# Projection weights in pieces of 1024 columns, and the residual additions on another engine, in a fused mixer and feed-forward kernel

## The chip, the cores and the metric

The kernel runs on one core of a Trainium2 chip. A core has five engines that run their own instruction streams in order and wait for each other on semaphores: TensorE (PE, matmuls and transposes; PEld is its weight load), VectorE (DVE), ScalarE (ACT), GpSimd (POOL) and SyncE (SP), which here issues every DMA transfer. The metric is the device time of one execution in microseconds. The kernel before takes 2879.96 us, the median of 3 runs (2878.36 to 2882.97).

## The reference

One layer of a trunk, on 2064 tokens (16 meta tokens and 2048 inputs) of width 1024, all in float32:

```python
h = rmsnorm(x, g_pre)
u, q, k, v, o, gi, gf, ga, gb = jnp.split(h @ w_in, IN_SPLITS, axis=-1)
y_a = gelu(s5_ssm(u, ...)); y_a = y_a * sigmoid(y_a @ w_glu)
y_b = head_norm(mlstm_chunkwise(q, k, v, gi, gf)) * sigmoid(o)
merged = sigmoid(ga) * (y_a @ w_a) + sigmoid(gb) * (y_b @ w_b)
x = x + rmsnorm(merged @ w_out, g_post)
# then the channel mixer
h = rmsnorm(x, g_pre); a = causal_dwconv(h @ w_gate, w_conv, b_conv)
return x + rmsnorm((gelu(a) * (h @ w_up)) @ w_down, g_post)
```

`w_glu` is 512 x 512, `w_a` and `w_b` are 512 x 1024, `w_out` is 1024 x 1024.

## The kernel before

A float32 product is made from three matmuls on rounded halves (`mm3`): each operand is split into a high part in a short float format and the low rest. The split of a weight piece is `split_w`: ScalarE copies the float32 piece `ws` into `wh` (line 140), VectorE subtracts to get `wl` (line 142, or line 144 where a factor is applied too). `load_w` puts the load of `ws` ahead of it (line 149). The three tiles `ws`, `wh` and `wl` lie in the pool `dw` with two buffers each, and every weight of the kernel goes through them: 1024 columns wide in the dense stages, 512 wide in the projections that the change touches.

The program goes through these stages. Up to about 978 us: the input projection, the state-space scan and the mLSTM, which leave `ya`, `yb`, the gates `gab_d` and so on in DRAM. From there to about 1464 us: four blocks `b` of 512 tokens (the first has two more), each with `glu(b)` (4 weight pieces), `branches(b)` (8 pieces of `w_b` and 8 of `w_a`, one pair for each 128 output channels `m`) and `out_proj(b)` (2 halves `nh` of 8 pieces `k`, each used for four tiles of 128 tokens, 12 matmuls of 512 columns). Then `out_post(b, i)` for each tile of 128 tokens: a norm (its power runs on GpSimd, line 105), a scaling on VectorE (line 1020), the addition of the residual `xt` (line 1021), and a store to `h1_d` (line 1022). The residual piece is loaded into `xh`, of which there are three buffers (line 1018). The posts of block `b - 1` are issued after the branches of block `b`, so they stand beside `out_proj(b)`; those of block 3 come at the end, and add on VectorE. `norm_block` turns `h1_d` into the transposed, normed `h2_d`.

The feed-forward part multiplies with a seven-product scheme, in two passes `p` over 1024 tokens each. Its operands are sums and differences of quarters of `h2_d`, loaded in halves `hf` into the `mk` tiles (three buffers, lines 1039 and 1040): `ops_first` makes three differences (lines 1058 to 1060) and splits four operands (lines 1047 and 1048), `ops_second` makes three more (lines 1072 to 1075). `ops_first(0)` stands in the program behind `out_proj(3)`, and its work is spread over `branches(3)` and `out_proj(3)`. The feed-forward units start at about 1464 us and run to about 2380; the down projection follows to the end.

The order of the instructions on each engine is not written out by hand: the framework sets it when the program is built, from a simulated timeline, and it is fixed from then on. A change of a size or of an engine in one stage thus reorders the stages around it.

Of the kernel before, what the change touches and what calls it, by code (L numbers as in the profile page):

```python
# [49 lines left out]
def mixer_ffn_kernel(  # L50
# [1 line left out]
    tc: tile.TileContext,  # L52
    x, meta, h0_t, g_mix_pre, g_mix_post, w_v, w_g, w_m, b_gates,
    lam_re, lam_im, log_dt, sb, sb_sw, sc, sc_sw, ssm_d,
    w_glu, conv_qk, b_qk, g_head, w_a, w_b, w_out,
    g_ffn_pre, g_ffn_post, w_gate, w_up, conv_f, b_f, w_down,
    out,
    stop=None,
# [855 lines left out]
    def glu(b):  # L914
        ts, n, pieces, rowt = blkC[b]
        yaT, yah, yal = ya[b]
        y2h, y2l = t4(4), t4(5)
        for m in range(4):
            wh, wl = load_w(dw, w_glu[m], 512)
            for p0, pn in pieces:  # L920
                ps = pst("mm", [128, pn])
                for k in range(4):
                    mm3(ps, wh[:, k], wl[:, k], yah[:, k, p0:p0 + pn], yal[:, k, p0:p0 + pn], k == 0, k == 3)
                tg = cr.tile([128, 512], F32, tag="tg", name="tg", bufs=2)
                S.activation(tg[:, :pn], ps, AF.Tanh, scale=0.5)
                V.scalar_tensor_tensor(tg[:, :pn], tg[:, :pn], 1.0, yaT[:, m, p0:p0 + pn], ALU.add, ALU.mult)
                S.activation(y2h[:, m, p0:p0 + pn], tg[:, :pn], AF.Copy)
                V.tensor_tensor(y2l[:, m, p0:p0 + pn], tg[:, :pn], y2h[:, m, p0:p0 + pn].bitcast(F32), ALU.subtract)
        y2[b] = (y2h, y2l)
# [16 lines left out]
    def branches(b):  # L946
        ts, n, pieces, rowt = blkC[b]
        y2h, y2l = y2[b]
        ybh, ybl = yb2[b]
        mh, ml = [t4(8), t4(9)], [t4(10), t4(11)]  # L950
        for m in range(8):
            bh, bl = load_w(dw, w_b[m], 512, 0.25)
            ah, al = load_w(dw, w_a[m], 512, 0.25)
            gat = cr.tile([128, 2, 514], F32, tag="gat", name="gat", bufs=2)
            P.dma_start(out=gat[:, 0, :n], in_=gab_d[m, :, ts:ts + n])
            P.dma_start(out=gat[:, 1, :n], in_=gab_d[8 + m, :, ts:ts + n])
            for p0, pn in pieces:
                pc = slice(p0, p0 + pn)
                pb = pst("mm", [128, pn])
                for k in range(4):  # L960
                    mm3(pb, bh[:, k], bl[:, k], ybh[:, k, pc], ybl[:, k, pc], k == 0, k == 3)
                V.scalar_tensor_tensor(gat[:, 1, pc], gat[:, 1, pc], 1.0, pb, ALU.add, ALU.mult)
                pa = pst("ac", [128, pn])
                for k in range(4):
                    mm3(pa, ah[:, k], al[:, k], y2h[:, k, pc], y2l[:, k, pc], k == 0, k == 3)
                V.scalar_tensor_tensor(gat[:, 0, pc], gat[:, 0, pc], 1.0, pa, ALU.add, ALU.mult)
                V.tensor_tensor(gat[:, 0, pc], gat[:, 0, pc], gat[:, 1, pc], ALU.add)
                mhm = mh[m // 4][:, m % 4, pc]
                S.activation(mhm, gat[:, 0, pc], AF.Copy)
                done = V.tensor_tensor(ml[m // 4][:, m % 4, pc], gat[:, 0, pc], mhm.bitcast(F32), ALU.subtract)  # L970
        mg[b] = (mh, ml)
        return done
# [3 lines left out]
    def out_proj(b):  # L976
# [3 lines left out]
        for nh in range(2):  # L980
# [1 line left out]
            for i, (c0, rows) in enumerate(rowt):  # L982
                pss[i] = pst("mm" if rows == 2 else "ac", [rows, 512])
            for k in range(KD):
                wh, wl = load_w(dw, w_out[k * 128:(k + 1) * 128, nh * 512:(nh + 1) * 512], 512)
                wh = wh.rearrange("p a b -> p (a b)")
                wl = wl.rearrange("p a b -> p (a b)")
                for i, (c0, rows) in enumerate(rowt):
                    mm3(pss[i], mh[k // 4][:, k % 4, c0:c0 + rows], ml[k // 4][:, k % 4, c0:c0 + rows], wh, wl,
                        k == 0, k == KD - 1)  # L990
# [9 lines left out]
    def out_post(b, i):  # L1000
# [11 lines left out]
        for hh in range(2):  # L1012
# [5 lines left out]
                P.dma_start(out=xt[:rows], in_=src[:, cs_])  # L1018
            o = o2[hh]
            V.scalar_tensor_tensor(o[:rows], o[:rows], rs[:rows], g2b[:rows, cs_], ALU.mult, ALU.mult)  # L1020
            (V if b == 3 else G).tensor_tensor(o[:rows], o[:rows], xt[:rows], ALU.add)
            P.dma_start(out=h1_d[ts + c0:ts + c0 + rows, cs_], in_=o[:rows])

    def norm_block(b, pl):
# [25 lines left out]
    def ops_first(p):  # L1050

        op = {n: (t4(2 * i), t4(2 * i + 1)) for i, n in enumerate((1, 6, 2, 7))}
        for hf in range(2):
            b11, b12 = op_load(p, hf, 0)
            op_split(op[1], p, hf, b11)
            b21, b22 = op_load(p, hf, 1)
            E = V if p else G
            E.tensor_tensor(b11, b12, b11, ALU.subtract)
            E.tensor_tensor(b12, b22, b12, ALU.subtract)
            E.tensor_tensor(b22, b22, b11, ALU.subtract)  # L1060
            op_split(op[6], p, hf, b22)
            op_split(op[2], p, hf, b21)
            op_split(op[7], p, hf, b12)
# [236 lines left out]
def layouts(i):  # L1300
# [7 lines left out]
    def stat(mat, k):  # L1308
# [26 lines left out]
        "sc": st(cre, cim),  # L1335
        "sc_sw": st(cim, cre),
        "ssm_d": a["ssm_d"][0].T,
        "w_glu": stat(a["w_ssm_glu"][0], 4),
        "conv_qk": conv(a["w_qk_conv"][0], 8),
        "b_qk": a["b_qk_conv"].reshape(8, 128).T,  # L1340
        "g_head": row("g_head_norm"),
        "w_a": stat(a["w_branch_ssm"][0], 4),
        "w_b": stat(a["w_branch_mlstm"][0], 4),
        "w_out": a["w_out"][0],
        "g_ffn_pre": a["g_ffn_pre"].reshape(8, 128).T,
        "g_ffn_post": row("g_ffn_post"),
# [27 lines left out]
```

## Time and profile before

The profiled execution took 2886.44 us, of which 2884.7 are the span from the first to the last instruction; the granted TensorE clock was 0.99 on average.

| | busy us | share of the span | instructions |
|---|---|---|---|
| TensorE, matmuls (PE) | 2794.8 | 97% | 15654 |
| TensorE, weight loads (PEld) | 2506.7 | 87% | 15654 |
| VectorE (DVE) | 1798.8 | 62% | 3508 |
| ScalarE (ACT) | 1047.4 | 36% | 1995 |
| GpSimd (POOL) | 183.2 | 6% | 257 |

A row of instructions reads: line of the kernel, engine, operation, output <- inputs by the program's names, shapes, count | busy us, mean ns of one | idle time of the engine just before them and what ended it. `A <- B` in a list of waits means that A waited for B. A time that stands in brackets behind a row of the timeline is the idle time before it, with what ended it. Of a wait for several things only the one that came last is named.

### The profile page before, as it was taken

How to read it: one execution, taken by the hardware profiler on the slowest of the kernel's cores; microseconds unless marked ns; L12 is line 12 of the kernel's file. 1: busy time of each engine (PE TensorE's matmuls, PEld its weight loads, DVE VectorE, ACT ScalarE, POOL GpSimd, SP SyncE). 2: the span in 40 equal slices, each digit the busy share in tenths (PEclk: the TensorE clock that was granted, in tenths of full speed). 3: DMA queues.
4: the chain of work that ended last, by engine and by line, in shares of the span. 5: the costliest groups of instructions: out<-in, count | busy, mean ns of one | idle time of the engine just before them, and what ended most of it. 6: DMA issues, size and time to landing. Idle time of an engine off the chain costs nothing.

```text
span 2884.7 us, 41374 instructions
## 1 busy us (share of the span) xinstructions
PE 2794.8 (97%) x15654; PEld 2506.7 (87%) x15654; DVE 1798.8 (62%) x3508; ACT 1047.4 (36%) x1995; POOL 183.2 (6%) x257
## 2 busy tenths in 40 slices
PE   8999999999999999998779999998999999999999
PEld 8999999999999987776579999996888888888887
DVE  4638897377555465576777777788777774224333
ACT  6102233233443444434344444444444443223221
POOL 1000000000000000212310000001000000000000
PEclk9999999999999999999989999999999999999999
DMA  8334453211454564676746222224222235334553
GB/s 303 105 73 137 169 162 117 74 69 70 147 158 134 159 200 134 196 221 219 234 142 201 80 81 84 71 82 175 81 84 78 87 98 179 95 99 146 166 168 125
DMA packets 328442, 389.74 MB, mean 135 GB/s; under 512 B 41569, under 2 KB 230390, under 8 KB 328114
## 3 DMA queue, kind: packets, MB, share of 16 engines
q1 hardware_dynamic: 328242, 387.10, 41.9%
q8 instruction: 123, 2.02, 0.3%
q14 instruction: 77, 0.63, 0.1%
HBM read 282.90 MB, written 104.12 MB: 134 GB/s over the span
## 4 chain that ended last, share of the span: by engine, by line
PE 83%; DMA 7%; DVE 6%; issue 2%; ACT 1%; POOL 1%; SPq 0%; POOLq 0%; DVEq 0%; ACTq 0%
PE mm L158 9%; PE mm L156 9%; PE mm L157 9%; PE ac L157 8%; PE ac L158 8%; PE ac L156 8%; PE ac L162 5%; PE ac L163 5%; PE ac L161 5%; PE mm L163 4%; PE mm L162 4%; PE mm L161 4%; DMA mk<-h_d 1%; DMA wo_d<-W 1%; DMA h_d<-mk 1%
## 5 line engine op out<-in xcount | busy, mean ns | idle before, releaser
L158 PE MATMUL mm<-hTh,wl 128*128 128x410 f32 (+3 forms) x1216 | 430.4, 354 | 0.0
L156 PE MATMUL mm<-hTh,wh 128*128 128x410 f32 (+3 forms) x1216 | 429.4, 353 | 0.1
L157 PE MATMUL mm<-hTl,wh 128*128 128x410 f32 (+3 forms) x1216 | 427.2, 351 | 0.0
L1275 DVE TENSOR_TENSOR yhl<-ys,yhl 128x1024 fp32r<-128x1024 f32 (+1 forms) x96 | 109.1, 1137 | 293.7 <-ACT yhl L1274 293.7
L157 PE MATMUL ac<-t,yhl 128*128 128x512 f32 x704 | 278.5, 396 | 0.0
L158 PE MATMUL ac<-t,yhl 128*128 128x512 f32 x704 | 277.3, 394 | 0.0
L156 PE MATMUL ac<-t,yhl 128*128 128x512 f32 x704 | 276.6, 393 | 0.0
L161 PE MATMUL mm<-t,w 128*128 128x258 f32 (+2 forms) x792 | 254.6, 322 | 12.6 <-ACT w L1142 9.7
L161 PE MATMUL ac<-t,w 128*128 128x258 f32 (+2 forms) x792 | 255.0, 322 | 12.1 <-ACT t L1047 8.0
L162 PE MATMUL mm<-t,w 128*128 128x258 f32 (+2 forms) x792 | 255.1, 322 | 1.3 <-DVE t L1048 1.3
L162 PE MATMUL ac<-t,w 128*128 128x258 f32 (+2 forms) x792 | 254.9, 322 | 1.1 <-DVE t L1048 1.1
L163 PE MATMUL mm<-t,w 128*128 128x258 f32 (+2 forms) x792 | 253.6, 322 | 1.7 <-DVE w L1143 1.7
L163 PE MATMUL ac<-t,w 128*128 128x258 f32 (+2 forms) x792 | 254.7, 322 | 0.0
L140 ACT ACTIVATE wh<-ws 128x512 fp32r<-128x512 f32 (+1 forms) x176 | 124.5, 708 | 317.7 <-PE mm L157 139.3
L156 PEld LDWEIGHTS mm<-hTh,wh 128*128 128x128 f32 x1216 | 229.2, 188 | 3.2 <-DVE ev L351 0.8
L157 PEld LDWEIGHTS mm<-hTl,wh 128*128 128x128 f32 x1216 | 229.2, 189 | 2.6
L158 PEld LDWEIGHTS mm<-hTh,wl 128*128 128x128 f32 x1216 | 229.2, 189 | 2.4
L1274 ACT ACTIVATE yhl<-ys 128x1024 fp32r<-128x1024 f32 (+1 forms) x96 | 94.8, 988 | 350.6 <-PE ac L157 349.0
L1142 ACT ACTIVATE w<-s 128x512 fp32r<-128x512 f32 x176 | 110.3, 630 | 192.5 <-PE ac L163 112.3
L161 PEld LDWEIGHTS mm<-t,w 128*128 128x128 f32 x792 | 151.0, 191 | 25.6 <-ACT w L1142 9.9
L161 PEld LDWEIGHTS ac<-t,w 128*128 128x128 f32 x792 | 150.7, 190 | 25.1 <-ACT t L1047 8.3
L142 DVE TENSOR_TENSOR wl<-ws,wh 128x512 fp32r<-128x512 f32 (+1 forms) x112 | 104.5, 936 | 108.4 <-ACT wh L140 108.1
(448 smaller groups left out, 6180.2 us busy)
## 6 DMA issues: line engine op xcount, KB each, us to landing
ys<-y_d SPq DMA_DIRECT2D x64, 512.0 KB, 3.7
wg<-in_w_gate_dram SPq DMA_DIRECT2D x44, 512.0 KB, 4.8
wu<-in_w_up_dram SPq DMA_DIRECT2D x44, 512.0 KB, 3.9
gab_d<-ev SPq DMA_DIRECT2D x80, 205.0 KB, 2.2
ws<-in_w_m_dram SPq DMA_DIRECT2D x32, 512.0 KB, 4.0
ws<-in_w_out_dram SPq DMA_DIRECT2D x64, 256.0 KB, 3.0
gat<-gab_d SPq DMA_DIRECT2D x48, 256.0 KB, 3.6
ys<-y_d SPq DMA_DIRECT2D x32, 384.0 KB, 3.1
```

Of the source, the lines that this page charges most:

```text
L140: S.activation(wh, ws, AF.Copy, scale=scale)
L142: V.tensor_tensor(wl, ws, wh.bitcast(F32), ALU.subtract)
L156: T.matmul(out=ps, lhsT=lh, rhs=rh, start=first, stop=False)
L157: T.matmul(out=ps, lhsT=lh, rhs=rl, start=False, stop=False)
L158: T.matmul(out=ps, lhsT=ll, rhs=rh, start=False, stop=last)
L161: T.matmul(out=ps, lhsT=lh, rhs=rh, start=first, stop=False, skip_group_check=True)
L162: T.matmul(out=ps, lhsT=lh, rhs=rl, start=False, stop=False, skip_group_check=True)
L163: T.matmul(out=ps, lhsT=ll, rhs=rh, start=False, stop=last, skip_group_check=True)
L1142: S.activation(t[:, 0], src, AF.Copy)
L1274: S.activation(yh, ys, AF.Copy)
L1275: V.tensor_tensor(yl, ys, yh.bitcast(F32), ALU.subtract)
```

## The change

It has two parts.

The weights of the three projections are fetched and split 1024 columns at a time. `w_glu` is laid out on the host so that two of its pieces lie side by side, and is loaded at every second `m`. `w_b` and `w_a` are joined into `w_ba`, one load for each `m`. Of `w_out` one transfer fetches two row blocks `k` side by side. There are half as many loads and splits (72 instead of 144), each of twice the width; the buffers stay two. The matmuls read the same halves of the same numbers.

The additions of two tensors on GpSimd move to VectorE: the residual addition of blocks 0 to 2 and the three differences of `ops_first(0)`, each done twice. What stays on GpSimd in these stages is the power of the norm and the small memsets.

```diff
         for m in range(4):
-            wh, wl = load_w(dw, w_glu[m], 512)
+            if m % 2 == 0:
+                w2h, w2l = load_w(dw, w_glu[m // 2], D)
+            wh, wl = (t[:, m % 2 * 4:m % 2 * 4 + 4] for t in (w2h, w2l))
...
         for m in range(8):
-            bh, bl = load_w(dw, w_b[m], 512, 0.25)
-            ah, al = load_w(dw, w_a[m], 512, 0.25)
+            bah, bal = load_w(dw, w_ba[m], D, 0.25)
+            (bh, bl), (ah, al) = ((bah[:, i:i + 4], bal[:, i:i + 4]) for i in (0, 4))
...
             for k in range(KD):
-                wh, wl = load_w(dw, w_out[k * 128:(k + 1) * 128, nh * 512:(nh + 1) * 512], 512)
-                wh = wh.rearrange("p a b -> p (a b)")
-                wl = wl.rearrange("p a b -> p (a b)")
+                if k % 2 == 0:
+                    ws = dw.tile([128, D], F32, tag="ws", name="ws")
+                    P.dma_start(out=ws.rearrange("p (k n) -> p k n", k=2),
+                                in_=w_out[k * 128:(k + 2) * 128, nh * 512:(nh + 1) * 512].rearrange(
+                                    "(k p) n -> p k n", k=2))
+                    w2 = split_w(dw, ws, D)
+                wh, wl = (t[:, k % 2 * 512:k % 2 * 512 + 512] for t in w2)
...
-            (V if b == 3 else G).tensor_tensor(o[:rows], o[:rows], xt[:rows], ALU.add)
+            V.tensor_tensor(o[:rows], o[:rows], xt[:rows], ALU.add)
...
-            E = V if p else G
-            E.tensor_tensor(b11, b12, b11, ALU.subtract)
-            E.tensor_tensor(b12, b22, b12, ALU.subtract)
-            E.tensor_tensor(b22, b22, b11, ALU.subtract)
+            V.tensor_tensor(b11, b12, b11, ALU.subtract)
+            V.tensor_tensor(b12, b22, b12, ALU.subtract)
+            V.tensor_tensor(b22, b22, b11, ALU.subtract)
```

In the changed kernel's listing the line numbers behind `glu` are higher: 1020 and 1021 become 1026 and 1027, 1022 and 1018 become 1028 and 1024, 1048 becomes 1054, 1058 to 1060 become 1063 to 1065, 1072 becomes 1077. The loads of `w_out` are at 989 instead of 149.

The first place where the order moves is VectorE beside `out_proj(3)`. `o` are the output tiles, `t` the operands of the feed-forward part, `mk` the halves of `h2_d`. Before, from the third split of a `w_out` piece on:

```order
L142 TENSOR_TENSOR wl<-ws,wh 128x512
L103 TENSOR_SCALAR ms<-sq 128x1
L142 TENSOR_TENSOR wl<-ws,wh 128x512
L1020 SCALAR_TENSOR_TENSOR o_12999<-o_12999,rs,g2b 128x512
L1020 SCALAR_TENSOR_TENSOR o_13155<-o_13155,rs,g2b 128x512
L103 TENSOR_SCALAR ms<-sq 128x1
L1048 TENSOR_TENSOR t_14244<-mk,t_14243 128x1028
L1072 TENSOR_TENSOR mk<-mk 128x2x514
L1048 TENSOR_TENSOR t_14240<-mk,t_14239 128x1028
L1048 TENSOR_TENSOR t_14242<-mk,t_14241 128x1028
L142 TENSOR_TENSOR wl<-ws,wh 128x512
```

Now, from the third split (of a piece of twice the width) to just ahead of the fourth:

```order
L142 TENSOR_TENSOR wl<-ws,wh 128x1024
L1065 TENSOR_TENSOR mk<-mk 128x2x514
L1026 SCALAR_TENSOR_TENSOR o_12699<-o_12699,rs,g2b 128x512
L1026 SCALAR_TENSOR_TENSOR o_12831<-o_12831,rs,g2b 128x512
L103 TENSOR_SCALAR ms<-sq 128x1
L1054 TENSOR_TENSOR t_13812<-mk,t_13811 128x1028
L1077 TENSOR_TENSOR mk<-mk 128x2x514
L1027 TENSOR_TENSOR o_12699<-o_12699,xh 128x512
L1054 TENSOR_TENSOR t_13808<-mk,t_13807 128x1028
L1027 TENSOR_TENSOR o_12831<-o_12831,xh 128x512
L1026 SCALAR_TENSOR_TENSOR o_12701<-o_12701,rs,g2b 128x512
L1026 SCALAR_TENSOR_TENSOR o_12833<-o_12833,rs,g2b 128x512
```

Two rows follow (`L103` and a fourth `L1054`), and then the fourth split. The additions `L1027` and the difference `L1065` stand now between two splits on the engine that makes the splits; a split covers twice as many matmuls.

The second place is SyncE's queue at the same point, where the h1 stores, the residual loads and the weight loads stand in one line. Before:

```order
L1022 DMA h_d<-o_12999 128x512
L1018 DMA xh<-in_x_dram 128x512
L1022 DMA h_d<-o_13155 128x512
L1018 DMA xh<-in_x_dram 128x512
L1040 DMA mk<-h_d 128x2x1026 x2
L149 DMA ws<-in_w_out_dram 128x512
L1022 DMA h_d<-o_13001 128x512
L1018 DMA xh<-in_x_dram 128x512
L149 DMA ws<-in_w_out_dram 128x512
```

Now:

```order
L989 DMA ws<-in_w_out_dram 128x2x512
L1046 DMA mk<-h_d 128x2x1026
L1028 DMA h_d<-o_12699 128x512
L1024 DMA xh<-in_x_dram 128x512
L1028 DMA h_d<-o_12831 128x512
L1024 DMA xh<-in_x_dram 128x512
L1046 DMA mk<-h_d 128x2x1026
L989 DMA ws<-in_w_out_dram 128x2x512
L1028 DMA h_d<-o_12701 128x512
L1024 DMA xh<-in_x_dram 128x512
L989 DMA ws<-in_w_out_dram 128x2x512
```

A store waits for its addition, and what stands behind it waits too. Five of the eight loads of `w_out` now stand ahead of the first store; before, six of the sixteen did, of half the width.

More of the change, by code (lines that the diff above doesn't have):

```diff
@@ L54, in mixer_ffn_kernel @@
     lam_re, lam_im, log_dt, sb, sb_sw, sc, sc_sw, ssm_d,
-    w_glu, conv_qk, b_qk, g_head, w_a, w_b, w_out,
+    w_glu, conv_qk, b_qk, g_head, w_ba, w_out,
     g_ffn_pre, g_ffn_post, w_gate, w_up, conv_f, b_f, w_down,
@@ L1337, in layouts @@
         "ssm_d": a["ssm_d"][0].T,
-        "w_glu": stat(a["w_ssm_glu"][0], 4),
+        "w_glu": stat(a["w_ssm_glu"][0], 4).reshape(2, 2, 128, 512).transpose(0, 2, 1, 3).reshape(2, 128, 1024),
         "conv_qk": conv(a["w_qk_conv"][0], 8),
@@ L1341, in layouts @@
         "g_head": row("g_head_norm"),
-        "w_a": stat(a["w_branch_ssm"][0], 4),
-        "w_b": stat(a["w_branch_mlstm"][0], 4),
+        "w_ba": np.concatenate([stat(a["w_branch_mlstm"][0], 4), stat(a["w_branch_ssm"][0], 4)], axis=2),
         "w_out": a["w_out"][0],
```

## The prediction

> **What bounds the kernel now.** I read the engines' shares first, then the chain of work that ended last. These two lines of the page say that TensorE (PE) sets the end:
>
> ```profile
> PE 2794.8 (97%) x15654; PEld 2506.7 (87%) x15654; DVE 1798.8 (62%) x3508; ACT 1047.4 (36%) x1995; POOL 183.2 (6%) x257
> ...
> PE 83%; DMA 7%; DVE 6%; issue 2%; ACT 1%; POOL 1%; SPq 0%; POOLq 0%; DVEq 0%; ACTq 0%
> ```
>
> The diff leaves the number of matmuls as it is, so time can come only from TensorE's gaps: 2884.7 - 2794.8 = 90 us of the span, and matmuls at a low clock beside them. The third view is busy time by stretches, cut at the stages of the projections (about 978 to 1464 us). The columns are the stretch, its width, busy us of PE, PEld, DVE, ACT and POOL with their counts, the clock granted to TensorE, the DMA share and GB/s.
>
> ```profile
> 978.00:1045.00 67.00, 62.11 (x485) 60.83 (x484) 49.27 (x109) 37.02 (x69) 0.00 (x0) 0.95 0.79 233
> 1045.00:1158.00 113.00, 112.59 (x511) 86.21 (x510) 55.89 (x93) 49.33 (x91) 0.00 (x0) 1.00 0.48 146
> 1158.00:1215.00 57.00, 52.76 (x228) 40.80 (x227) 32.95 (x54) 18.53 (x34) 19.33 (x15) 1.00 0.68 217
> 1215.00:1270.00 55.00, 54.83 (x252) 43.14 (x251) 39.13 (x68) 29.80 (x59) 3.05 (x5) 1.00 0.62 193
> 1270.00:1335.00 65.00, 58.99 (x267) 46.34 (x266) 38.58 (x65) 24.64 (x46) 18.02 (x19) 1.00 0.81 259
> 1335.00:1400.00 65.00, 57.55 (x233) 43.85 (x232) 45.71 (x60) 28.33 (x51) 10.46 (x4) 0.97 0.50 165
> 1400.00:1464.00 64.00, 49.97 (x196) 38.07 (x195) 36.59 (x45) 20.15 (x32) 21.72 (x18) 0.89 0.67 226
> 1464.00:1500.00 36.00, 20.73 (x130) 19.94 (x129) 32.85 (x56) 18.05 (x38) 8.28 (x6) 0.72 0.46 161
> 2000.00:2100.00 100.00, 100.00 (x432) 80.93 (x431) 72.33 (x113) 40.69 (x65) 4.56 (x5) 1.00 0.25 85
> ```
>
> The gaps lie where POOL has work: the stretches with 10 to 22 us of POOL lack 4.2, 6.0, 7.5 and 14.0 us of PE, while 1045 to 1158 and 1215 to 1270, with 0 and 3 us of it, lack 0.4 and 0.2. The last row prices an undisturbed matmul of 512 columns: 100 / 432 = 0.2315 us. The stretches 1335 to 1400 and 1400 to 1464 hold only such matmuls, so they need 233 x 0.2315 = 53.9 and 196 x 0.2315 = 45.4 us: 11.1 and 18.6 us are lost there, the lower clock included. What TensorE waits for from 960 to 1620 (us, times, longest):
>
> ```profile
> PE ac L157 <- DVE wl L142: 11.8, 8, 4.8
> PE mm L161 <- ACT w L1142: 9.7, 1, 9.7
> PE ac L156 <- ACT wh L140: 8.1, 6, 2.8
> PE mm L156 <- ACT wh L140: 5.0, 7, 2.3
> ...
> PE ac L161 <- ACT u L1185: 3.9, 1, 3.9
> ```
>
> The first, third and fourth are the split weight pieces, 24.9 us; the 9.7 and the 3.9 belong to the start of the feed-forward units behind 1464.
>
> Why pieces come late is in the timeline. One POOL row (a pair of L1058), then VectorE's rows under it, and one row from later for comparison:
>
> ```profile
> 1355.99 5.34 POOL L1058 TENSOR_TENSOR mk<-mk 128x1028 f32<-128x1028 f32 x2 [25.35 <-DVE t L1048]
> ```
>
> ```profile
> 1359.39 2.50 DVE L967 TENSOR_TENSOR gat<-gat 128x512 f32<-128x512 f32 x1
> 1361.80 0.67 DVE L962 SCALAR_TENSOR_TENSOR gat<-gat,mm 128x512 f32<-128x512 f32 x1
> 1362.40 2.26 DVE L144 SCALAR_TENSOR_TENSOR wl<-ws,wh 128x512 fp32r<-128x512 f32 x1
> ...
> 1382.08 0.68 DVE L144 SCALAR_TENSOR_TENSOR wl<-ws,wh 128x512 fp32r<-128x512 f32 x1
> ```
>
> Beside POOL's additions a VectorE instruction with two SBUF inputs takes 2.3 to 2.5 us instead of 0.68; L962, which reads one input from PSUM, keeps 0.67. The Trainium skill ("SBUF — State Buffer", Who interferes with whom) says the same: such an instruction and a GpSimd one that reads SBUF exclude each other, and the later one blocks. By that page alone the moved additions' whole time could be VectorE time given back, which leads to the first rival below; the groups' rows bound it lower.
>
> The second cause is SyncE's queue. In out_proj(3) ScalarE stood 13.28 us for a weight piece, and the queue had stood for POOL's additions (here the waits of SP from 1400 to 1464):
>
> ```profile
> 1429.67 0.63 ACT L140 ACTIVATE wh<-ws 128x512 fp32r<-128x512 f32 x1 [13.28 <-DMA ws<-in_w_out_dram]
> ```
>
> ```profile
> SPq L1022 <- POOL o L1021: 9.9, 5, 4.3
> ```
>
> **The additions.** POOL loses these groups (978 to 1500; 2 more of two rows):
>
> ```profile
> L1021 POOL TENSOR_TENSOR o<-o,xh 128x512 f32<-128x512 f32 x24 | 38.9, 1633 | 14.4 <-DVE o L1020 10.6 <-DMA xh<-in_x_dram 2.8 <-issue 1.1
> L1058 POOL TENSOR_TENSOR mk<-mk 128x1028 f32<-128x1028 f32 x2 | 5.3, 2693 | 25.4 <-DVE t L1048 25.4
> L1059 POOL TENSOR_TENSOR mk<-mk 128x1028 f32<-128x1028 f32 x2 | 5.2, 2616 | 3.6 <-DMA mk<-h_d 3.6
> L1060 POOL TENSOR_TENSOR mk<-mk 128x1028 f32<-128x1028 f32 x2 | 4.3, 2168 | 0.1
> ```
>
> VectorE's prices (978 to 1600):
>
> ```profile
> L142 DVE TENSOR_TENSOR wl<-ws,wh 128x512 fp32r<-128x512 f32 x79 | 64.8, 823 | 105.1 <-ACT wh L140 104.9
> L144 DVE SCALAR_TENSOR_TENSOR wl<-ws,wh 128x512 fp32r<-128x512 f32 x64 | 46.8, 731 | 14.6 <-ACT wh L140 14.0
> L1020 DVE SCALAR_TENSOR_TENSOR o<-o,rs,g2b 128x512 f32<-128x512 f32 x32 | 24.3, 800 | 8.8 <-POOL rs L105 8.8
> L1021 DVE TENSOR_TENSOR o<-o,x 128x512 f32<-128x512 f32 x8 | 5.2, 685 | 0.0
> L1072 DVE TENSOR_TENSOR mk<-mk 128x1028 f32<-128x1028 f32 x2 | 4.6, 2302 | 0.0
> L1074 DVE TENSOR_TENSOR mk<-mk 128x1028 f32<-128x1028 f32 x2 | 2.5, 1227 | 0.2 <-DMA mk<-h_d 0.2
> ```
>
> Added: 26 x 0.685 + 6 x 1.227 = 25 us. Given back against the undisturbed 0.685 and 1.227: 79 x 0.138 + 64 x 0.046 + 32 x 0.115 + 2 x 1.075 = 10.9 + 2.9 + 3.7 + 2.2 = 20 us, and a few more in smaller groups. VectorE's load stays even. What changes is latency: an addition of 1.6 us becomes 0.7, and the h1 store and the x load behind it leave SyncE that much sooner. The price: VectorE is in order, so where an x piece or an h2 half hasn't landed, the splits behind it wait too.
>
> **The pieces.** Undisturbed 1024-column pieces (dense stages, 300 to 980), the 512-column one of this stage, and three loads:
>
> ```profile
> L142 DVE TENSOR_TENSOR wl<-ws,wh 128x1024 fp32r<-128x1024 f32 x23 | 28.1, 1222 | 2.4 <-ACT wh L140 2.4
> ```
>
> ```profile
> L140 ACT ACTIVATE wh<-ws 128x1024 fp32r<-128x1024 f32 x23 | 24.4, 1061 | 30.0 <-PE mm L157 30.0
> ```
>
> ```profile
> L140 ACT ACTIVATE wh<-ws 128x512 fp32r<-128x512 f32 x143 | 89.9, 630 | 192.9 <-DMA ws<-in_w_out_dram 77.3 <-PE ac L158 40.0 <-PE ac L157 21.1
> ```
>
> ```profile
> ws<-in_w_m_dram SPq DMA_DIRECT2D x32, 512.0 KB, 4.0
> ws<-in_w_out_dram SPq DMA_DIRECT2D x64, 256.0 KB, 3.0
> xh<-in_x_dram SPq DMA_DIRECT2D x24, 256.0 KB, 4.8
> ```
>
> There are two buffers of each kind before and after. A piece's split can start when the piece two back is used up, and must be done when the one between is: 12 x 0.2315 = 2.78 us before, of which 0.63 + 0.69 = 1.3 is work, so 1.5 us of delay was free. Now it is 5.56 us, less 1.06 + 1.22 = 2.3: 3.3 us is free. The load behind it is covered by 5.56 us for 4.0 instead of 2.78 for 3.0. The work of the splits is the same.
>
> **The sum.** Out_proj(3), 18.6 lost. The longest VectorE run between two splits in the new order is L1065, four L1026, three L1054, L1077 and two L1027: 5 x 1.227 + 6 x 0.685 = 10.2 us, with the split itself 11.5. It has 5.56 + 3.3 = 8.9 of cover, so it stalls TensorE 2.6 us; I add 2 for the powers on GpSimd (a pair of L1026 waits for one) and for ScalarE, and 1.5 at low clock. Some 6 us stay, 12.5 are won. Glu and branches(3), 11.1 lost: the run is two L1054, four of L1063 to L1065 and an L972, 6 x 1.227 + 0.685 = 8.0 us, behind two pieces already split (11.1 us of matmuls), which stalls nothing; I leave 3.5 for the stage's head and win 7.5. The two earlier out_projs, 10.2 of plain gaps: a run of eight 512-column instructions is 5.5 us, two powers lengthen it by about 2, against 3.3 free; half stays, 5 are won. The head (978 to 1045, 4.9 missing) and the feed-forward start (15.3 missing) have the same instructions in nearly the same order: 0, with 3 us either way. Together 25 us: the profiled execution's 2886.4 becomes 2861, and the median of the runs, 2880.0 (6.4 below the profiled one), becomes **2855 us**.
>
> Ends for what the trace doesn't show: the standing of VectorE at its new loads costs nothing if each lands in time, and at most 26 us (the last rival); the removed contention is worth at least the 4.2 + 6.0 gaps' half and at most everything that is missing.
>
> **The rivals.** *More comes back.* All of 11.1 + 18.6 + 10.2 = 40 us goes and the feed-forward start shrinks by 4, since VectorE reaches it earlier: 2836. For it: 1045 to 1158 shows these stages with no gap. Against it: the run of 11.5 us. *The heads pay.* At the start of a stage nothing is split ahead; a piece's first matmul then comes (4.0 - 3.0) + (1.06 - 0.63) + (1.22 - 0.69) = 2 us later. With 12 heads (glu, branches and out_proj of four blocks) that is 24 us, which cancels the gain: 2879. Against it: the next stage's first pieces stand directly behind the last w_out piece in SyncE's order. The Trainium skill ("Perfetto Trace Analysis", Optimizing Scalar/DVE Operations) speaks for this one: where these engines aren't saturated but cause bubbles elsewhere, it advises smaller instructions, and the change makes larger ones; VectorE is at 62%. *VectorE waits in POOL's place (slower).* An x buffer comes round after addition, issue and landing, 0.7 + 0.7 + 4.8 = 6.2 us for three additions, and VectorE's work for three is 6 x 0.685 = 4.1; 26 / 3 rounds stand 2.1 us each, 18 us, and the h2 halves that POOL awaited 3.6 us stand twice, 7: 26 us with the splits behind them. Of the gain only the deeper prefetch stays, some 14 of the three weight waits' 24.9: 2880 + 12 = 2892. It decides once over 14 us of that standing reaches TensorE. Against it: the first three x pieces are loaded ahead, and two buffered pieces cover 8.9 us.
>
> **How the numbers follow.** Forecast 0.62 (its own range 2845 to 2867), more comes back 0.15, the heads pay 0.16, VectorE waits 0.07. The 8-in-10 range is 2836 to 2874: it takes in the second case and half of the way to the third. A measurement here tells 0.2% (5.8 us) from no change. Faster by more than that: 0.62 + 0.15 + a third of the heads' 0.16 = 0.82; within it 0.10; slower 0.08, the last rival with a rest of the heads'.
>
> **What would show it.** Right: no L1021-like rows on POOL; two-input VectorE rows at 0.69 and 1.22 throughout; TensorE short of less than 4 us in glu and branches(3) and of about 5 in out_proj(3); ScalarE's wait for w_out far below 13 us; the span up to 978 and behind 1600 as before. Wrong: VectorE idle before its additions for x loads by more than 10 us in all, TensorE's waits for wl as long as now, or a feed-forward start longer by what was won.

## The result, and the profile after

The changed kernel takes 2849.84 us, the median of 4 runs (2847.5 to 2852.07), against 2879.94 us for the kernel before on the same chip (4 runs, 2878.36 to 2882.97): a ratio of 0.9894, with a 95% interval of 0.9877 to 0.9911. The change is worth 30.1 us; the forecast was 25 (2855 us). The profiled execution took 2852.07 us, of which 2850.3 are the span, 34.4 less than the span before. The two profiled executions lie 6.5 us (before) and 2.2 us (now) above the medians of their kernels, so 4.3 of these 34.4 us are a difference of executions and not of kernels.

These are the engines' shares and the chain of waits of the changed kernel, from its page:

```profile
PE 2785.3 (98%) x15654; PEld 2509.1 (88%) x15654; DVE 1790.8 (63%) x3468; ACT 1035.4 (36%) x1923; POOL 132.0 (5%) x225
...
PE 84%; DMA 7%; DVE 6%; issue 1%; ACT 1%; POOL 0%; SPq 0%; DVEq 0%; POOLq 0%; ACTq 0%
```

GpSimd lost 51 us of work, VectorE gained none (1798.8 before, 1790.8 now), and TensorE's gaps went from 90 to 65 us. To see where, I cut both spans at the same events: the end of ScalarE's last eviction in `out_proj(0)`, `(1)` and `(2)`, and the first feed-forward matmul. Between two of these lie the posts, `out_proj`, `glu` and branches of one block. The busy time by such stretches, of the kernel before and then of the changed one (the columns are those of the prediction's table of stretches):

```profile
1109.30:1218.50 109.20, 104.55 (x448) 81.47 (x447) 67.75 (x108) 49.50 (x92) 19.33 (x15) 1.00 0.62 193
1218.50:1335.80 117.30, 111.12 (x506) 87.28 (x505) 77.62 (x132) 51.92 (x99) 21.06 (x24) 1.00 0.74 235
1335.80:1464.40 128.60, 107.12 (x425) 81.60 (x424) 82.70 (x105) 48.08 (x82) 32.19 (x22) 0.93 0.58 193
sum 355.10, PE 322.78 PEld 250.35 DVE 228.07 ACT 149.50 POOL 72.57; mean PE 107.59 PEld 83.45 DVE 76.02 ACT 49.83 POOL 24.19
```

```profile
1104.90:1211.20 106.30, 103.36 (x453) 82.83 (x452) 68.49 (x101) 46.03 (x73) 5.99 (x5) 1.00 0.65 203
1211.20:1322.00 110.80, 108.12 (x485) 86.95 (x484) 74.06 (x116) 48.43 (x82) 8.07 (x13) 0.98 0.69 226
1322.00:1430.90 108.90, 104.09 (x445) 83.26 (x444) 80.36 (x109) 45.12 (x64) 9.74 (x11) 0.97 0.70 244
sum 326.00, PE 315.56 PEld 253.03 DVE 222.91 ACT 139.58 POOL 23.79; mean PE 105.19 PEld 84.34 DVE 74.30 ACT 46.53 POOL 7.93
```

The three blocks together have nearly as many matmuls as before (1379 and 1383 recorded), and take 355.1 - 326.0 = 29.1 us less: 2.9, 6.5 and 19.7. Their gaps fell from 32.3 to 10.4 us. Ahead of 1109 us 4.4 us were won, behind the feed-forward start 0.9 (1420.3 us to the end before, 1419.4 now).

What TensorE waits for in the changed kernel from 960 to 1590 (us, times, longest):

```profile
PE ac L161 <- ACT u L1190: 8.6, 2, 6.4
PE mm L161 <- ACT w L1147: 5.9, 1, 5.9
PE ac L157 <- DVE wl L142: 5.6, 5, 3.5
...
PE ac L158 <- DVE wl L144: 0.7, 1, 0.7
PE ac L156 <- ACT wh L140: 0.5, 1, 0.5
```

The waits for split weight pieces, 24.9 us in the forecast's count, are 5.6 + 0.7 + 0.5 = 6.8 us. (The count before left out the waits for the subtractions with a factor, line 144: 4.8 us, which the 6.8 take in. With them it was 29.7.) What stands first now is the feed-forward start, which the change did not touch.

VectorE's groups in the changed kernel from 978 to 1466 us show what became of the stretched rows:

```profile
L142 DVE TENSOR_TENSOR wl<-ws,wh 128x1024 fp32r<-128x1024 f32 x39 | 47.6, 1221 | 73.5 <-ACT wh L140 73.5
L144 DVE SCALAR_TENSOR_TENSOR wl<-ws,wh 128x1024 fp32r<-128x1024 f32 x32 | 39.1, 1222 | 16.2 <-ACT wh L140 16.2
L1026 DVE SCALAR_TENSOR_TENSOR o<-o,rs,g2b 128x512 f32<-128x512 f32 x32 | 22.6, 745 | 2.9 <-POOL rs L105 2.0 <-POOL mk L1045 0.9
...
L1027 DVE TENSOR_TENSOR o<-o,xh 128x512 f32<-128x512 f32 x24 | 16.3, 685 | 8.7 <-DMA xh<-in_x_dram 8.7
```

Each of these groups of two-input rows is at its undisturbed time (1.22, 0.745, 0.685), and VectorE's standing for the residual loads is 8.7 us in all.

The one long wait that is left is the predicted one. VectorE's rows between the third and the fourth split of `out_proj(3)`, and the matmul behind:

```profile
1388.79 1.22 DVE L142 TENSOR_TENSOR wl<-ws,wh 128x1024 fp32r<-128x1024 f32 x1
1389.92 1.23 DVE L1065 TENSOR_TENSOR mk<-mk 128x1028 f32<-128x1028 f32 x1
1391.58 1.41 DVE L1026 SCALAR_TENSOR_TENSOR o<-o,rs,g2b 128x512 f32<-128x512 f32 x2 [0.44 <-POOL rs L105]
...
1400.13 1.22 DVE L142 TENSOR_TENSOR wl<-ws,wh 128x1024 fp32r<-128x1024 f32 x1
```

```profile
1401.40 0.79 PE L157 MATMUL ac<-wl,t 128*128 128x512 f32 x1 [3.54 <-DVE wl L142]
```

From split to split it is 11.3 us (11.5 forecast), and TensorE stands 3.54. Two stretches of the changed kernel, `out_proj(3)` from its first matmul to the feed-forward start, and the 6 us behind that wait:

```profile
1380.10:1430.90 50.80, 47.26 (x193) 37.91 (x192) 35.65 (x53) 20.28 (x28) 9.43 (x8) 0.93 0.78 275
1401.40:1407.40 6.00, 6.00 (x15) 4.70 (x16) 4.36 (x7) 0.60 (x1) 3.00 (x3) 0.52 0.61 193
```

Its 192 matmuls need 192 x 0.2315 = 44.4 us, so 6.4 are lost: 3.5 in the wait, and 6.0 - 15 x 0.2315 = 2.5 behind it, where the granted clock is 0.52.

### The profile page after: what moved, and what is told of

Same layout as the page of the kernel before. It is cut to its first block, busy times and chain, and to the rows that moved or that the text cites. A ratio compares the mean times of both kernels' runs of the same rounds, so it can differ in the third digit from the quotient of the medians.

```text
span 2850.3 us, 40942 instructions
## 1 busy us (share of the span) xinstructions
PE 2785.3 (98%) x15654; PEld 2509.1 (88%) x15654; DVE 1790.8 (63%) x3468; ACT 1035.4 (36%) x1923; POOL 132.0 (5%) x225
## 4 chain that ended last, share of the span: by engine, by line
PE 84%; DMA 7%; DVE 6%; issue 1%; ACT 1%; POOL 0%; SPq 0%; DVEq 0%; POOLq 0%; ACTq 0%
PE mm L156 9%; PE mm L158 9%; PE mm L157 9%; PE ac L157 9%; PE ac L158 9%; PE ac L156 9%; PE ac L161 5%; PE ac L163 5%; PE ac L162 5%; PE mm L162 4%; PE mm L163 4%; PE mm L161 4%; DMA gat<-gab_d 1%; DMA wo_d<-W 1%; DMA h_d<-mk 1%
## 5 line engine op out<-in xcount | busy, mean ns | idle before, releaser
L1280 DVE TENSOR_TENSOR yhl<-ys,yhl 128x1024 fp32r<-128x1024 f32 (+1 forms) x96 | 109.2, 1138 | 295.3 <-ACT yhl L1279 295.3
L140 ACT ACTIVATE wh<-ws 128x1024 fp32r<-128x1024 f32 x104 | 109.8, 1058 | 239.4 <-PE mm L157 140.1
L1147 ACT ACTIVATE w<-s 128x512 fp32r<-128x512 f32 x176 | 110.4, 631 | 202.5 <-PE ac L163 119.3
L161 PEld LDWEIGHTS ac<-t,w 128*128 128x128 f32 x792 | 151.1, 191 | 30.0 <-ACT u L1190 9.7
L162 PEld LDWEIGHTS ac<-t,w 128*128 128x128 f32 x792 | 151.6, 191 | 13.3 <-DVE t L1054 1.8
```

The source lines that it names most:

```text
L140: S.activation(wh, ws, AF.Copy, scale=scale)
L161: T.matmul(out=ps, lhsT=lh, rhs=rh, start=first, stop=False, skip_group_check=True)
L162: T.matmul(out=ps, lhsT=lh, rhs=rl, start=False, stop=False, skip_group_check=True)
L1147: S.activation(t[:, 0], src, AF.Copy)
L1280: V.tensor_tensor(yl, ys, yh.bitcast(F32), ALU.subtract)
```

## The experiments

All runs beside the kernel before on the same chip, in three groups with a before of their own (2883.74, 2881.45 and 2881.21 us). The gain is the difference of the medians.

| run | us, median (range) | ratio to before (95%) | gain |
|---|---|---|---|
| pieces only | 2861.11 (2858.06 to 2864.65) | 0.9924 (0.9912 to 0.9936) | 22.6 |
| additions only | 2869.51 (2866.42 to 2874.71) | 0.9953 (0.9941 to 0.9966) | 14.2 |
| residual additions only | 2873.23 (2872.02 to 2873.35) | 0.9963 (0.9949 to 0.9977) | 10.5 |
| idle additions on GpSimd | 2862.58 (2857.33 to 2864.17) | 0.9924 (0.9912 to 0.9937) | 21.2 |
| split in halves | 2849.87 (2846.41 to 2855.38) | 0.9888 (0.9871 to 0.9905) | 31.6 |
| stores on another queue | 2877.35 (2875.0 to 2880.63) | 0.9985 (0.9976 to 0.9993) | 4.1 |
| differences on GpSimd | 2852.47 (2847.53 to 2855.4) | 0.989 (0.9872 to 0.9908) | 29.0 |
| later norms and evictions | 2841.24 (2837.72 to 2844.28) | 0.9856 (0.984 to 0.9872) | 40.2 |
| changed kernel again | 2850.04 (2846.39 to 2855.08) | 0.989 (0.9873 to 0.9907) | 31.2 |
| wide pieces for w_out only | 2855.22 (2852.86 to 2855.78) | 0.9906 (0.9892 to 0.9921) | 26.0 |
| later norms only | 2843.18 (2840.64 to 2846.78) | 0.9867 (0.9852 to 0.9882) | 38.0 |
| norms apart | 2843.59 (2842.1 to 2848.01) | 0.987 (0.9855 to 0.9885) | 37.6 |

The same cuts as above, from each run's trace, in us. Single executions of one kernel differ by some us (the changed kernel's runs reach from 2846.4 to 2855.1), so differences of 2 or 3 here say nothing alone. The last two columns belong together: a run that is longer in block 3 is often shorter behind it (the pieces alone have 9.6 us more than the changed kernel in block 3 and 7.5 less from the feed-forward start).

| run | end of out_proj(0) | block 1 | block 2 | block 3 | from the feed-forward start |
|---|---|---|---|---|---|
| before | 1109.3 | 109.2 | 117.3 | 128.6 | 1420.3 |
| changed | 1104.9 | 106.3 | 110.8 | 108.9 | 1419.4 |
| changed again | 1103.0 | 107.9 | 110.7 | 108.2 | 1419.5 |
| pieces only | 1105.6 | 111.1 | 112.2 | 118.5 | 1411.9 |
| additions only | 1106.0 | 108.6 | 114.3 | 120.6 | 1418.0 |
| residual additions only | 1105.3 | 107.0 | 115.0 | 128.4 | 1415.8 |
| idle additions | 1101.5 | 113.6 | 113.1 | 116.9 | 1416.5 |
| split in halves | 1102.9 | 102.7 | 108.2 | 117.2 | 1419.3 |
| another queue | 1106.4 | 108.3 | 118.2 | 122.8 | 1417.5 |
| differences on GpSimd | 1104.3 | 108.1 | 110.4 | 111.9 | 1418.9 |
| later norms and evictions | 1100.0 | 107.3 | 110.8 | 107.9 | 1416.3 |
| w_out only | 1106.9 | 105.0 | 112.2 | 114.9 | 1414.8 |
| later norms only | 1100.2 | 108.0 | 111.6 | 106.6 | 1414.4 |
| norms apart | 1105.4 | 105.9 | 112.1 | 109.1 | 1413.6 |

### Each part alone

The pieces alone are the changed kernel with both additions back:

```diff
-            V.tensor_tensor(o[:rows], o[:rows], xt[:rows], ALU.add)
+            (V if b == 3 else G).tensor_tensor(o[:rows], o[:rows], xt[:rows], ALU.add)
...
-            V.tensor_tensor(b11, b12, b11, ALU.subtract)
+            E = V if p else G
+            E.tensor_tensor(b11, b12, b11, ALU.subtract)
```

(with the other two differences alike). Expected:

> The changed kernel with the additions of the residual and of the three differences back on GpSimd; the pieces stay 1024 wide. The forecast's theory: three causes, of which this leaves one removed, the shallow prefetch. The three weight waits of TensorE were 24.9 us before; the deeper prefetch is worth some 14 of them (the figure of the last rival), so about 2866; VectorE's two-input rows beside GpSimd's additions stay at 1.5 to 2.5 us. Rival A, depth is all: the pieces alone give the whole 30 us, 2850, and the stretched rows don't matter since a split covers 5.56 us of matmuls. Rival B, GpSimd is all: no gain, 2875 to 2880, since a wider split beside an addition is stretched by the same factor as two narrow ones.

The additions alone are the kernel before with these lines the other way round. Expected:

> The kernel before with both groups of additions on VectorE; the pieces stay 512 wide. The forecast's theory: contention and the standing of SyncE's queue are gone, 1.5 us of free delay per piece remain, and the runs of VectorE instructions between two splits (5.5 to 10 us) now meet the shallow prefetch: about half of the gain, 2864. Rival A, depth is all: nothing, 2878 or more, since a run of eight 512-column instructions (5.5 us) stalls TensorE by some 2 us wherever it stands. Rival B, GpSimd is all: the whole gain, 2850.

Measured: 22.6 and 14.2 us. Neither rival holds: both parts give something alone, the pieces more than I had put on them (22.6 instead of 14), the additions somewhat less (14.2 instead of 16). Their sum is 36.8, more than the 30 or 31 of both together, so some 6 us are waits that either part removes. In the trace of the pieces alone, VectorE's rows beside GpSimd's additions in `out_proj(3)`, TensorE's wait for them, and the group of the scalings from 1050 to 1460 us:

```profile
1405.61 3.15 DVE L1026 SCALAR_TENSOR_TENSOR o<-o,rs,g2b 128x512 f32<-128x512 f32 x2 [4.09 <-POOL rs L105]
...
1408.75 2.25 DVE L1054 TENSOR_TENSOR t<-mk,t 128x1028 fp32r<-128x1028 f32 x1
1410.93 2.32 DVE L1078 TENSOR_TENSOR mk<-mk 128x1028 f32<-128x1028 f32 x1
...
1416.84 4.43 DVE L142 TENSOR_TENSOR wl<-ws,wh 128x1024 fp32r<-128x1024 f32 x2
```

```profile
PE ac L157 <- DVE wl L142: 7.3, 1, 7.3
```

```profile
L1026 DVE SCALAR_TENSOR_TENSOR o<-o,rs,g2b 128x512 f32<-128x512 f32 x29 | 23.3, 843 | 19.8 <-POOL rs L105 19.4 <-POOL mk L1045 0.4
```

Two of the 1.22 us rows take 2.25 and 2.32, and the run to the fourth split, which is shorter than in the changed kernel by two additions and a difference, costs TensorE 7.3 us instead of 3.5. From the third split to the fourth it is 16.5 us, where its instructions undisturbed need 8.6 (the changed kernel's 11.3 less the two additions, the difference and 0.44 of standing): 3.9 are stretched rows, and 4.1 are VectorE's standing for one power. That power runs on GpSimd, which is in order: it stands behind a difference there, and the difference behind the load of its `h2` half. In all VectorE stands 19.4 us for powers in this kernel, and 2.0 in the changed one. So moving the additions takes away two things, the stretching and the powers' place behind the additions; the prediction has the second only as about 2 us for the powers. Two pieces ahead cover 8.9 us, not a run lengthened by both.

### The residual additions alone

The kernel before with only the line of the residual addition changed to VectorE. Expected:

> The kernel before with the 24 residual additions on VectorE, the differences on GpSimd, the pieces 512 wide. The two earlier out_projs and the SyncE queue in out_proj(3) are relieved, the contention of the three differences in branches(3) and out_proj(3) stays. Forecast's theory: about two thirds of what the additions alone give, some 10 us, 2870. Rival: the differences carry it (a pair of 5.3 us stands beside glu and branches(3), where 11.1 us were lost), and this run gains under 4 us, 2876 or more.

Measured: 10.5 us, as expected. But not where: block 3 has 128.4 us, as before (128.6), while the additions with the differences have 120.6. With narrow pieces the differences do hold up block 3. Where the 10.5 us of the residual additions come from stays open: in the traces blocks 1 and 2 are shorter by 4.5 us, the rest of the difference lies ahead of the first of these additions and behind the feed-forward start, and each part is of the size by which executions differ.

### Contention without anybody waiting

The changed kernel, and on GpSimd beside each residual addition one into a scratch tile that has no reader (so this kernel does 24 additions that its result doesn't use):

```diff
             V.tensor_tensor(o[:rows], o[:rows], xt[:rows], ALU.add)
+            if b < 3:
+                G.tensor_tensor(scr[:rows], o[:rows], g2b[:rows, cs_], ALU.add)
```

> The changed kernel, and beside each of the 24 residual additions on VectorE an addition of the same size on GpSimd (the scaled tile plus a constant row, into a scratch tile that nobody reads). Nothing waits for GpSimd, so SyncE's queue is as in the changed kernel; only the contention comes back. If contention is the larger part of what the residual additions cost: VectorE rows beside them at 1.5 to 2.5 us and 24 x about 1.2 us of VectorE time, of which half reaches TensorE: 10 us or more slower than the changed kernel, 2860 to 2865. If the queue or the depth is the larger part: under 4 us slower, 2850 to 2854.

Measured: 21.2 us faster than before, 9 to 10 slower than the changed kernel, near the first expectation, and as slow as the pieces alone (their ranges lie over each other). The groups of this kernel from 1050 to 1460 us, VectorE's and then GpSimd's, and TensorE's wait from 960 to 1600:

```profile
L142 DVE TENSOR_TENSOR wl<-ws,wh 128x1024 fp32r<-128x1024 f32 x36 | 47.6, 1322 | 66.1 <-ACT wh L140 65.9
L1026 DVE SCALAR_TENSOR_TENSOR o<-o,rs,g2b 128x512 f32<-128x512 f32 x30 | 36.5, 1256 | 1.5 <-POOL rs L105 1.5
...
L1027 DVE TENSOR_TENSOR o<-o,xh 128x512 f32<-128x512 f32 x24 | 20.3, 870 | 0.4 <-DMA xh<-in_x_dram 0.3
```

```profile
L1027 POOL TENSOR_TENSOR scr<-o,g2b 128x512 f32<-128x512 f32 x24 | 39.2, 1634 | 11.2 <-DVE o L1027 9.8 <-DVE ms L103 0.7
```

```profile
PE ac L157 <- DVE wl L142: 17.1, 9, 4.8
```

39.2 us of additions that nobody needs lengthen VectorE by 30 x 0.511 + 36 x 0.101 + 24 x 0.185 = 15.3 + 3.6 + 4.4 = 23 us, and TensorE's wait for split pieces goes from 5.6 to 17.1. VectorE's busy time in all rises as much, from 1790.8 to 1812.7 us. With wide pieces, then, the contention of these 24 additions costs some 9 us, though nothing waits for their results. What follows from it is in this price: SyncE's queue was expected to be as in the changed kernel, but its stores stand 41.7 us for VectorE's additions (19.9 there), since VectorE comes to them later. That the pieces alone are as slow doesn't show that waiting for GpSimd costs nothing: VectorE makes 24 additions fewer there (16 us), and stands 19.4 us for powers (1.5 here). The rule for the contention is that of the Trainium skill ("SBUF — State Buffer", Who interferes with whom), that a VectorE instruction with two SBUF inputs and a GpSimd one that reads SBUF exclude each other; the trace agrees, with 1.256 for 0.745 us. The build sets its own order for this kernel, so that a part of the 9 us can be order.

### The standing queue

The kernel before, with GpSimd instead of SyncE issuing the stores and residual loads of the first three blocks:

```diff
-                P.dma_start(out=xt[:rows], in_=src[:, cs_])
+                G.dma_start(out=xt[:rows], in_=src[:, cs_])
...
-            P.dma_start(out=h1_d[ts + c0:ts + c0 + rows, cs_], in_=o[:rows])
+            (P if b == 3 else G).dma_start(out=h1_d[ts + c0:ts + c0 + rows, cs_], in_=o[:rows])
```

> The kernel before, with the h1 stores and the residual loads of blocks 0 to 2 issued by GpSimd instead of SyncE: SyncE's queue no longer stands for GpSimd's additions (23.9 us in 17 waits from 978 to 1466), the additions, their contention and the 512-wide pieces stay. If the standing queue is half of what the additions cost (they gave 14 us alone): 5 to 8 us faster than before. If contention is nearly all of it, as the idle additions suggest: under 3 us faster, or slower by what issuing 34 stores and 26 loads costs GpSimd.

Measured: 4.1 us, between the two expectations (26 stores and 26 loads move; the 34 of the expectation take in block 3's stores). What SyncE waited for from 1050 to 1466 us in the kernel before, in this one, and (978 to 1430) in the changed one:

```profile
SPq L149 <- DVE wl L142: 98.4, 51, 5.5
...
SPq L1022 <- POOL o L1021: 23.9, 17, 4.3
```

```profile
SPq L149 <- DVE wl L142: 125.3, 63, 5.4
...
SPq L1040 <- POOL mk L1039: 20.0, 5, 8.9
```

```profile
SPq L1028 <- DVE o L1027: 19.9, 15, 2.8
```

The wait of the stores for GpSimd is gone here. A longer wait for the weight buffers, which come free when a split is done, stands in its place, and another wait for GpSimd: before the load of an `h2` half SyncE waits for a small memset on GpSimd (line 1039), which stands behind GpSimd's other work, 20.0 us instead of 4.9. So this run moved the standing on GpSimd more than it took it away, and its 4.1 us do not price the queue. Two other runs say more about it. ScalarE's longest wait for a `w_out` piece in `out_proj(3)`, 13.28 us in the kernel before, in this run and with the additions alone:

```profile
1422.38 0.63 ACT L140 ACTIVATE wh<-ws 128x512 fp32r<-128x512 f32 x1 [11.87 <-DMA ws<-in_w_out_dram]
```

```profile
1418.96 0.63 ACT L140 ACTIVATE wh<-ws 128x512 fp32r<-128x512 f32 x1 [11.80 <-DMA ws<-in_w_out_dram]
```

With the additions alone no store waits for GpSimd, and ScalarE still stands 11.8 us. With the pieces alone SyncE stands 15.1 us there for GpSimd's additions, and ScalarE waits 0.6 us for a load. So ScalarE's 13 us went with the narrow pieces, and not with the stores' wait for GpSimd's additions, as I had taken it. In the changed kernel the stores still hold the queue 19.9 us, 4.6 of them in `out_proj(3)` (9.9 before).

### The differences

The changed kernel with the three differences back on GpSimd, as in the diff of the pieces alone, the residual additions on VectorE. Expected:

> The changed kernel with the three differences of the first feed-forward operands back on GpSimd (each twice, 14.8 us of it), the residual additions on VectorE. Theory: they stretch two-input VectorE rows by 1.8 us each in branches(3) and out_proj(3) and bring back some of the wait before the fourth w_out piece, but the difference leaves the 11.3 us run between two splits (one of 1.22 us): 3 to 6 us slower than the changed kernel. Rival: with two 1024-wide pieces ahead the stretch is covered, and the shorter run pays: within 2 us of it.

Measured: 29.0 us, 1 to 2 us less than the changed kernel's gains (30.1 and 31.2), and 2847.53 to 2855.4 us lies over its range. The rival holds: with two wide pieces ahead this part of the change is worth nothing that can be told.

### Depth or size

The changed kernel, each piece split by two instructions on each engine into the same buffers:

```diff
-        S.activation(wh, ws, AF.Copy, scale=scale)
+        for c in (slice(i * n // parts, (i + 1) * n // parts) for i in range(parts)):
+            S.activation(wh[:, c], ws[:, c], AF.Copy, scale=scale)
```

(the subtraction alike, with `parts` 2 in the three projections). Expected:

> The changed kernel, its loads and buffers 1024 wide, but each piece split by two instructions of 512 columns on ScalarE and two on VectorE. It tells the depth of the prefetch from the size of the instruction. Theory, depth: the buffers hold as much ahead as in the changed kernel, and a half costs 0.63 + 0.69 as before, so within 3 us of the changed kernel (30 us faster than before). Rival, the heads pay: a piece's first matmul comes 1 us sooner here (0.43 on ScalarE, 0.53 on VectorE), and other work slips between the halves, so 5 us or more faster than the changed kernel. Other side: 71 more instructions on VectorE at 2 x 0.685 - 1.222 = 0.15 us each, 11 us more work; if VectorE's load reaches TensorE, 4 us or more slower than the changed kernel.

Measured: 31.6 us, the time of the changed kernel. So the size of a split instruction is not what the wide pieces give; what is left is how far ahead the pieces are loaded and split. The size and number of the loads went with that depth in every run (512 KB, half as many), so these two are not told apart: no run has four buffers of 512 columns. VectorE's busy time is 1793.3 us, 2.5 more than in the changed kernel, where the expectation priced 11. The advice of the Trainium skill to break up instructions that cause bubbles on another engine ("Perfetto Trace Analysis", Optimizing Scalar/DVE Operations) finds no support here: at the same depth half the size is neither faster nor slower. The order of the program changes with it (block 1 and 2 are shorter, block 3 is longer), so this holds for the sum only.

### Where the width matters

The changed kernel with `glu` and branches back at 512 columns:

```diff
-            bah, bal = load_w(dw, w_ba[m], D, 0.25)
-            (bh, bl), (ah, al) = ((bah[:, i:i + 4], bal[:, i:i + 4]) for i in (0, 4))
+            bh, bl = load_w(dw, w_ba[m][:, 0:512], 512, 0.25)
+            ah, al = load_w(dw, w_ba[m][:, 512:D], 512, 0.25)
```

> The changed kernel with the pieces of the glu and the branches back at 512 columns; those of the out_proj stay 1024 wide, all additions on VectorE. If the depth matters where the posts' work lies between the splits (the out_projs held 28.8 of the 39.9 us lost): within 3 us of the changed kernel. If the narrow pieces of branches(3), with six differences and eight splits of the feed-forward operands beside them, stall again: 5 to 8 us slower than it.

Run beside it, the changed kernel itself:

> The changed kernel itself, beside the next three on the same chip, so that they can be compared with it directly: 30 us faster than the kernel before.

Measured: 26.0 and 31.2 us. The moved additions and the wide `w_out` pieces give 26 together, 12 more than the additions alone in their group; the narrow pieces of `glu` and branches cost 5, and block 3 is 114.9 us for 108.2. That is at the lower edge of the second expectation.

### A faster version

The feed-forward start stood first in the changed kernel's waits, and the 64 us behind its first 36 lacked 4.3. The norms that make the second pass's operands were put later:

```diff
-        if m == 1:
+        if m == 3:
             norm_block(2, dsm)
             norm_block(3, dsm)
```

and in a first run ScalarE also took all evictions of the last `out_proj`:

```diff
-                if b == 3 and nh and i % 2:
+                if False:
```

> An attempt at a faster kernel, from the changed one: the norms of blocks 2 and 3 come behind the feed-forward unit 3 instead of 1, and ScalarE evicts all four tiles of the last out_proj (two were VectorE's). In the changed kernel the stretch from 36 to 100 us behind the feed-forward start lacks 4.3 us of TensorE (2.1 of it transposes that wait for VectorE) and the first 36 us lack 15.3, with VectorE busy for 32.6 of them. If VectorE's load there is the cause: 4 us from the norms and 1 from the evictions, 35 us faster than the kernel before. If the transposes only wait for the order of the store and load behind them: no difference, 30 us faster.

> Of the faster attempt the one half: the norms of blocks 2 and 3 behind unit 3, the evictions as in the changed kernel. If the norms carry the gain, as the full stretch of 64.0 of 64 us behind the first 36 us says: 35 to 40 us faster than the kernel before, no slower than the attempt with both. If the evictions carry it: 30 to 33.

> The norms of block 2 behind unit 3, those of block 3 behind unit 6. In the attempt with both behind unit 3 one transpose still waits 2.2 us for VectorE. If four tiles of norms at a time fit between a unit's work: 2 us faster than with both behind unit 3. If the wait is that of one transpose for its own chain, whatever stands beside it: the same.

Measured: 40.2, 38.0 and 37.6 us. Beside the changed kernel's 2850.04 on the same chip the norms alone have 2843.18, so the later norms are worth 7 us by the medians; in the traces 5.1 of the 8.5 us between the two lie behind the feed-forward start, and 2.8 ahead of the end of `out_proj(0)`, where the edit has no instruction. The evictions add nothing that ranges as wide as these can tell, and putting the two norms apart adds nothing. The two stretches behind the feed-forward start, of the changed kernel and of the later norms alone:

```profile
1431.00:1467.00 36.00, 20.65 (x131) 19.61 (x130) 32.56 (x53) 16.93 (x35) 9.41 (x7) 0.76 0.48 161
1467.00:1531.00 64.00, 59.70 (x497) 59.16 (x496) 53.18 (x108) 27.32 (x51) 6.16 (x10) 0.99 0.54 165
```

```profile
1427.00:1463.00 36.00, 21.46 (x131) 20.47 (x131) 32.51 (x54) 16.64 (x33) 9.37 (x7) 0.76 0.47 161
1463.00:1527.00 64.00, 64.00 (x539) 64.00 (x538) 53.89 (x108) 28.16 (x51) 3.02 (x6) 1.00 0.31 100
```

The second stretch is full, with 42 matmuls more; the first is as it was. This version, 2841 to 2843 us, beats both kernels. That the norms' work was in the way is not shown by it alone: with the pieces alone the same 64 us are full too (64.00 of 64), with the norms at their old place, so the order that the build sets can be a part of this.

## Why the prediction was right, point by point

**What bounds the kernel, and where the gaps lie.** Right: 29.1 of the span's 34.4 us were won in the three blocks that had GpSimd's additions, 19.7 of them in the last.

**Out_proj(3): 12.5 to win, 6 to stay.** From its first matmul (1400.8 before, 1380.1 now) to the feed-forward start it took 63.6 and takes 50.8 us: 12.8 won, 6.4 stay. The parts are right in kind, a little off in size: the stall 3.5 for 2.6, the low clock 2.5 for 1.5. The 2 for the powers and ScalarE, which no row showed, was not needed; the power's 0.44 us lies inside the run. The run has three L1054, as the sum counts them (under the change the last of them is called the fourth). The changed kernel's second trace has a stall of 3.1 us at the same wait.

**Glu and branches(3): 7.5 to win.** From 65.0 to 58.1 us, 6.9 won, though 21 transposes (3.1 us) came into this stretch from block 2. For equal work it is 10.0, and little more than 1 us of gaps stays (58.1 less 56.8 of TensorE): the 3.5 left for the stage's head were not needed. The width counts there: with narrow pieces in `glu` and branches block 3 is longer by 6.7 us.

**The earlier out_projs: 5 to win.** This term was too small: blocks 1 and 2 became shorter by 9.4. Of their plain gaps, 10.8 before by these cuts, 5.2 went, as the term said; but it counted plain gaps alone, and 4.2 us of TensorE's busy time went as well. A part of this is work that moved: of the 72 transposes (`tp`) that stood in block 2, 21 stand in block 3 now, 2.6 us of TensorE in block 2 and 3.1 in block 3, and five others (0.7 us) came into block 1 from ahead of it. For equal work blocks 1 and 2 became shorter by 9.4 - 2.6 + 0.7 = 7.5 us, and block 3 by 19.7 + 3.1 = 22.8.

**The head: 0, with 3 either way.** The end of `out_proj(0)`, ahead of which GpSimd has no additions, came 4.4 us earlier. In the nine traces with wide pieces in `glu` and branches it lies at 100.0 to 105.6 (1100 taken off), mean 103.1, in the five with narrow ones at 105.3 to 109.3, mean 106.8. Counted from the first matmul of `glu(0)`, ahead of which the kernels are alike, it comes after 124.1 to 126.5 us in the nine and after 129.1 to 130.6 in the five. So about 4 us come from the wide pieces of `glu` and branches here too, and the head pays nothing: it gains. To put this stretch at nothing was the sum's one mistake of kind. By the spans, block 3's 19.7 are what was forecast (12.5 + 7.5), which is in part luck, since 3.1 us of work came in; the 4.4 here and the 4.4 too little for blocks 1 and 2 make 34.4 of 25 between the profiled executions, with the feed-forward part's 0.9. Between the medians it is 30.1, so the terms as measured here are too large by some 4 us together.

**The three causes.** Contention and depth were right; the queue, as it was told, was not. "ScalarE's wait far below 13 us" did come (its longest for a piece in `out_proj(3)` is 3.2 us), but the pieces alone bring it too, with SyncE standing for GpSimd as before, and the additions alone don't. A fourth cause was put at part of 2 us that stay: the powers, which stand behind the additions on GpSimd and hold up VectorE's scalings (8.8 us in all before, 19.4 with the pieces alone, 2.0 now). The depth was priced too low for a cause alone: 22.6 instead of some 14, load size included.

**VectorE's load even.** Right, and it decided that the additions could move at all: 1798.8 before, 1790.8 now. The idle additions show why: 24 of them on GpSimd cost VectorE 23 us, more than the 24 x 0.685 = 16 that it needs to do them. The wider splits help as well: one of 1.22 us takes the place of two of 0.685.

**The rivals.** *The heads pay* falls with the earlier end of `out_proj(0)` and with the split in halves. *VectorE waits in POOL's place*: it stands 8.7 us for the residual loads and 2.9 for an `h2` half, 12 of the 26 priced, below the 14 from which it was to decide; in the run behind TensorE's longest wait VectorE stands for a power alone, 0.44 us. *More comes back* needed a shorter feed-forward start; that did not come by itself (0.9 us), and in the last experiment another edit brought it.

## What to carry to other kernels

Before moving work off GpSimd or back, compare what its rows cost VectorE with what the work itself costs there: a helper engine that stretches the busy one by as much as it relieves it is no help, even where nobody waits for it. Look also at what stands behind that work in the helper's own stream. Where an in-order engine prepares operands between other work, look for its longest run between two preparations, and make what is prepared ahead cover that run; in these runs the width of an instruction mattered less than the depth. Count matmuls at a low clock behind a stall as part of the stall.

## What the runs showed of the hardware

GpSimd is held up beside VectorE too, which I had not looked for. GpSimd's power of 128 x 1, beside VectorE's run in `out_proj(3)` of the changed kernel, and the durations of that line from 978 to 1466 us (min, median, max, ns):

```profile
1388.95 2.60 POOL L105 TENSOR_TENSOR rs<-ms,neghalf 128x1 f32<-128x1 f32 x1 [2.61 <-DVE ms L103]
...
1399.22 4.27 POOL L105 TENSOR_TENSOR rs<-ms,neghalf 128x1 f32<-128x1 f32 x1 [4.56 <-DVE ms L103]
```

```profile
L105 POOL TENSOR_TENSOR rs<-ms,neghalf x27: 540/861/4270, 1170.9 to 1464.5; 128x1 f32<-128x1 f32 x25, 2x1 f32<-2x1 f32 x2
```

An instruction of 0.54 us takes up to 4.27 where VectorE issues one two-input instruction after another. The norms of the posts wait for it, 2.0 us of VectorE's time in the changed kernel, so the powers are a thing to look at there; no run here moved them.

A stall of 3.5 us cost 6.0 in all: the 15 matmuls behind it took 0.40 us each instead of 0.2315, at a granted clock of 0.52 over those 6 us.
